# Seven products in place of eight for gate and up in two feed-forwards

## The chip, the cores and the metric

The kernel runs on one core of one Trainium2 chip. The metric is device time in microseconds for one execution, lower is better.

## The reference, cut to what matters

A two-layer backbone over 256 latent tokens and 256 context tokens, model width 1024. Each layer is a half-step SwiGLU feed-forward, a mixer of three kinds of attention, and a second half-step feed-forward; all in float32. The last layer's second feed-forward needs latent tokens alone, so three of the four feed-forwards work on all 512 tokens.

```
def _swiglu(u, w_gate, w_up, w_down):          # u: tokens x 1024, hidden width 2816
    return (jax.nn.silu(u @ w_gate) * (u @ w_up)) @ w_down
h  = h  + 0.5 * g1  * _swiglu(_modulate(_rms_norm(h,  norm_ffn1[l]), sh1,  sc1),  ...)
hc = hc + 0.5 * cg1 * _swiglu(_modulate(_rms_norm(hc, norm_ffn1[l]), csh1, csc1), ...)
```

Shifts, scales and gates (`sh1`, `sc1`, `g1`, ...) come from a product of the silu of a conditioning vector with `w_ada`, 9 x 1024 outputs per layer for each of the two kinds of tokens.

## The kernel before, in words

Activations stand with model rows on the 128 partitions and tokens along the free dimension: `H` is 8 row tiles of 512 columns, latent (`LAT`) in the first 256 and context (`CT`) in the others. Float32 accuracy comes from three matmuls in a reduced format for each product (`mm3`): every weight tile and every activation is split into a high part (a copy by ScalarE) and a low part (a subtraction by VectorE), and high x high, high x low and low x high are added in PSUM. `wload` loads a weight tile of 128 x 1024 by SP's queue into one of three `raw` buffers and splits it into one of four `split` buffers.

`ffn` loops over 22 tiles of 128 hidden rows. `up_one` computes gate and up of one tile: 2 matrices x 8 row tiles x 3 matmuls of 512 columns (256 in the last feed-forward), then `evac` makes silu(gate) x up and its split `G`. `PARTS` groups the tiles by 6, 6, 6 and 4; after the first tile of the next group, `down` projects a whole group: for each of the 8 output tiles `d` a weight load, n x 3 matmuls, and `accum`, in which VectorE adds the gated PSUM half to `H`. The last group is done by halves of the tokens with 256 columns, so that the next norm starts early (`finish`).

Between tiles `run_jobs` issues jobs for the shifts, scales and gates of later stages: each loads 512 KB of `w_adaT` by GpSimd's queue into one of eight `araw` buffers, and VectorE reduces it once for each kind of token (`ada_dve`). The fourth feed-forward has no jobs. The order of work on each engine is set when the program is built, by a scheduler that takes ready instructions in program order; the first tiles and the mixers' steps are ordered by hand. Banks of PSUM: three for `mm`, two for `s` (gates), two for `t` (ups), one for `o`.

Of the kernel before, what the change touches and what calls it, by code (L numbers as in the profile page):

```python
# [13 lines left out]
ALU = mybir.AluOpType  # L14
# [7 lines left out]
PARTS = (6, 6, 6, 4)  # L22
A_H, B_H, C_H = 6, 4, 6
ABUFS = 8
# [36 lines left out]
def hybrid_backbone(ctx: ExitStack, tc: tile.TileContext, I, out):  # L61
# [45 lines left out]
    def late_consts_():  # L107
# [3 lines left out]
        late["maskC"] = const("maskC", [128, 2, 256], I["maskC"])  # L111
# [21 lines left out]
    def mm3(ps, wh, wl, xh, xl, first, last):  # L133
        mm(ps, wh, xh, start=first, stop=False)  # L134
        mm(ps, wh, xl, start=False, stop=False)  # L135
        mm(ps, wl, xh, start=False, stop=last)  # L136

    def proj(ps, sp, U, cols, nk=KT, off=0, k0=0, ks=None):
        for k in ks or range(nk):
            o = off + k * 128  # L140
            mm3(ps, sp[:, 0, o:o + 128], sp[:, 1, o:o + 128], U[0][:, k0 + k, cols], U[1][:, k0 + k, cols],
                k == 0, k == nk - 1)


    def ada_dve(l, ft, cb, ntok, pool):
        raw = pool.tile([128, 1024], F32, tag="araw", name="araw", bufs=ABUFS)
# [3 lines left out]
        for t in range(ntok):  # L150
            stt(scr, raw, 1.0, cb[:, t, :], op0=ALU.mult, op1=ALU.mult, accum_out=ada[l][:, ft, t:t + 1])  # L151
# [84 lines left out]

    def finish(halves, piece, gate, after):
# [23 lines left out]
    def first_tiles(pool, csel, U, src):  # L261
# [14 lines left out]
        def a(p, i):  # L276
# [4 lines left out]
            raw = pool.tile([128, 4, 256], F32, tag="araw", name="araw", bufs=ABUFS)  # L281
# [20 lines left out]
        def w(i):  # L302
            raw = raw_load(src(i), 1024)
            if i < 4:
                t = wp.tile([128, 2, 1024], F32R, tag="split", name="split", bufs=4)
                parts = [(t, 0, 1024)]
            else:
                parts = [(pool.tile([128, 2, 512], F32R, tag="G", name="split0", bufs=10), o, 512) for o in (0, 512)]
            for t, o, n in parts:
                act(t[:, 0, :], raw[:, o:o + n], AF.Copy)  # L310
            sps.append((raw, parts))

        def x(i):
            raw, parts = sps[i]
            for t, o, n in parts:
                tt(t[:, 1, :], raw[:, o:o + n], t[:, 0, :].bitcast(F32), ALU.subtract)
# [19 lines left out]
        def m(i, f):  # L336
            t, o, _ = sps[i][1][f // 4 if i >= 4 else 0]
            wh, wl = (t[:, e, f * 128 - o:f * 128 - o + 128] for e in range(2))
# [11 lines left out]
    def ffn(l, w, halves, pool, U, jobs, after, start=None):  # L350
        both = len(halves) == 2
# [7 lines left out]
        def run_jobs(frac):  # L359
# [589 lines left out]
```

## Time and profile before

| | us |
|---|---|
| median of 3 runs | 1743.18 (1739.81 to 1744.08) |
| the profiled execution | 1742.45 |
| its span, first to last instruction | 1740.5 |
| TensorE busy | 1700.8 (98%) |
| VectorE busy | 1180.0 (68%) |
| ScalarE busy | 718.5 (41%) |
| GpSimd busy | 165.8 (10%) |

The span is what the profiler saw of one execution; its own time stands beside it. Busy time is the time in which an engine had at least one instruction running. Matmuls overlap, so their cost is read from the distance between starts and not from their length.

### The profile page before, as it was taken

The numbers are of one execution on the slowest core, as the hardware profiler recorded it, in microseconds if no ns is written. First come the engines' busy times: TensorE is split into PE (matmuls) and PEld (weight loads), VectorE is DVE, ScalarE is ACT, GpSimd is POOL, SyncE is SP. The second block draws the span as 40 slices with busy tenths as digits, with TensorE's granted clock in tenths as the row PEclk, the third lists the DMA queues.
The fourth block names the chain that finished last, engine by engine and source line by source line (L and its number), as shares of the span: only waits on it lengthen the run. The fifth ranks groups of instructions, "written<-read, shape, count | busy, mean of one in ns | idle before, by whom it ended". The sixth has DMA issues, their size and how long they took to land.

```text
span 1740.5 us, 24756 instructions
## 1 busy us (share of the span) xinstructions
PE 1700.8 (98%) x9572; PEld 1477.5 (85%) x9572; DVE 1180.0 (68%) x2031; ACT 718.5 (41%) x1206; POOL 165.8 (10%) x251
## 2 busy tenths in 40 slices
PE   7999999999999999999999999999999999989997
PEld 4888888889888898888888898888888888889997
DVE  5899963447978869983334599934343787965555
ACT  4322222235888653222222442222222577754443
POOL 0311100012102031100000212100000211100000
PEclk9999999999999999999999999999999999989999
DMA  8877643323223247743333288824332333356663
GB/s 330 309 240 243 197 117 84 110 73 115 58 82 85 75 169 238 236 129 89 108 85 109 63 319 277 321 79 115 85 109 86 99 84 102 109 155 182 182 176 113
DMA packets 76693, 258.37 MB, mean 148 GB/s; under 512 B 8944, under 2 KB 11248, under 8 KB 76192
## 3 DMA queue, kind: packets, MB, share of 16 engines
q1 hardware_dynamic: 54096, 176.72, 33.2%
q0 software_dynamic: 21760, 79.38, 14.3%
q8 instruction: 75, 1.23, 0.3%
q10 hardware_dynamic: 720, 0.69, 0.1%
q14 instruction: 42, 0.34, 0.1%
HBM read 250.47 MB, written 1.05 MB: 145 GB/s over the span
## 4 chain that ended last, share of the span: by engine, by line
PE 89%; DVE 4%; ACT 4%; issue 2%; POOL 1%; DMA 1%; POOLq 0%; DVEq 0%; SPq 0%; ACTq 0%
PE pd L135 8%; PE pd L134 8%; PE pd L136 8%; PE pu L134 8%; PE pu L135 8%; PE pu L136 8%; PE pg L134 8%; PE pg L136 8%; PE pg L135 8%; PE pq L136 1%; PE pq L134 1%; PE pq L135 1%; PE pt L679 1%; DVE split L130 1%; PE pv L580 1%
## 5 line engine op out<-in xcount | busy, mean ns | idle before, releaser
L129 ACT ACTIVATE split<-raw 128x1024 fp32r<-128x1024 f32 (+1 forms) x336 | 332.7, 991 | 546.6 <-PE pu L136 223.2
L130 DVE TENSOR_TENSOR split<-raw,split 128x1024 fp32r<-128x1024 f32 (+1 forms) x336 | 383.9, 1143 | 234.1 <-ACT split L129 233.2
L151 DVE SCALAR_TENSOR_TENSOR ascr<-araw,cb 128x1024 f32<-128x1024 f32 x224 | 273.3, 1220 | 9.9 <-ACT cb L804 7.0
L135 PE MATMUL pd<-G,split 128*128 128x512 f32 (+1 forms) x800 | 272.5, 341 | 0.0
L134 PE MATMUL pd<-G,split 128*128 128x512 f32 (+1 forms) x800 | 271.5, 341 | 0.0
L136 PE MATMUL pd<-G,split 128*128 128x512 f32 (+1 forms) x800 | 271.4, 340 | 0.0
L134 PE MATMUL pg<-Uh,split 128*128 128x512 f32 (+1 forms) x712 | 252.4, 355 | 2.1 <-ACT Uh L225 2.1
L136 PE MATMUL pg<-Uh,split 128*128 128x512 f32 (+1 forms) x712 | 252.3, 354 | 0.0
L135 PE MATMUL pg<-Ul,split 128*128 128x512 f32 (+1 forms) x712 | 252.0, 355 | 0.1
L134 PE MATMUL pu<-Uh,split 128*128 128x512 f32 (+1 forms) x712 | 252.1, 354 | 0.0
L135 PE MATMUL pu<-Ul,split 128*128 128x512 f32 (+1 forms) x712 | 251.9, 354 | 0.0
L136 PE MATMUL pu<-Uh,split 128*128 128x512 f32 (+1 forms) x712 | 251.9, 354 | 0.0
L234 DVE SCALAR_TENSOR_TENSOR H<-pd,ada,H 128x256 f32<-128x256 f32 x272 | 123.3, 479 | 106.9 <-PE pd L136 106.8
L135 PEld LDWEIGHTS pd<-G,split 128*128 128x128 f32 x800 | 151.6, 190 | 17.2
L136 PEld LDWEIGHTS pd<-G,split 128*128 128x128 f32 x800 | 151.4, 190 | 16.9
L134 PEld LDWEIGHTS pd<-G,split 128*128 128x128 f32 x800 | 151.1, 189 | 17.3
L134 PEld LDWEIGHTS pg<-Uh,split 128*128 128x128 f32 x712 | 135.4, 190 | 21.0 <-ACT Uh L225 2.6
L135 PEld LDWEIGHTS pg<-Ul,split 128*128 128x128 f32 x712 | 135.4, 190 | 18.6 <-DVE Ul L226 0.3
L136 PEld LDWEIGHTS pu<-Uh,split 128*128 128x128 f32 x712 | 135.2, 190 | 18.5
L136 PEld LDWEIGHTS pg<-Uh,split 128*128 128x128 f32 x712 | 135.2, 190 | 18.4
L134 PEld LDWEIGHTS pu<-Uh,split 128*128 128x128 f32 x712 | 135.3, 190 | 18.3
L135 PEld LDWEIGHTS pu<-Ul,split 128*128 128x128 f32 x712 | 135.0, 190 | 18.4
(199 smaller groups left out, 2412.6 us busy)
## 6 DMA issues: line engine op xcount, KB each, us to landing
araw<-in_w_adaT POOLq DMA_DIRECT2D x128, 512.0 KB, 5.0
raw<-in_w_ffn_gate SPq DMA_DIRECT2D x88, 512.0 KB, 3.8
raw<-in_w_ffn_up SPq DMA_DIRECT2D x88, 512.0 KB, 3.9
raw<-in_w_ffn_down SPq DMA_DIRECT2D x96, 384.0 KB, 3.2
raw<-in_w_in SPq DMA_DIRECT2D x26, 512.0 KB, 3.5
araw<-in_w_ada SPq DMA_DIRECT2D x16, 512.0 KB, 9.9
raw<-in_w_ffn_down SPq DMA_DIRECT2D x16, 512.0 KB, 3.6
raw<-in_w_out SPq DMA_DIRECT2D x16, 512.0 KB, 3.7
```

Of the source, the lines that this page charges most:

```text
L129: act(sp[:, 0, :n], raw[:, :n], AF.Copy)
L130: tt(sp[:, 1, :n], raw[:, :n], sp[:, 0, :n].bitcast(F32), ALU.subtract)
L134: mm(ps, wh, xh, start=first, stop=False)
L135: mm(ps, wh, xl, start=False, stop=False)
L136: mm(ps, wl, xh, start=False, stop=last)
L151: stt(scr, raw, 1.0, cb[:, t, :], op0=ALU.mult, op1=ALU.mult, accum_out=ada[l][:, ft, t:t + 1])
L234: stt(H[:, d, cols], ps[:, off:off + 256], gate[:, d, half:half + 1], H[:, d, cols], op0=ALU.mult, op1=ALU.add)
L580: mm(ps[:, :n], U[0][:, k, c], s[:, 0, o:o + n], start=(k == 0), stop=False)
L679: nc.tensor.transpose(pt[:, k * 128:(k + 1) * 128], P[t][:, k * 128:(k + 1) * 128], ident)
```

## The change

In the second feed-forward of layer 0 and the first of layer 1 (`FAST`), tiles from 10 on are taken in pairs by `up_fast`. The activations are cut into four blocks (lower and upper four row tiles x latent and context tokens) and the weights of a pair into four blocks (lower and upper rows x gate and up), and the 2 x 2 block product is made of seven block products in place of eight. Each product has 2 x 4 x 3 matmuls of 256 columns. VectorE combines weight blocks before the split and results after the product. Sums of activation blocks (`S1` to `S3`) are made in `forms` after tile 5, `S4` in `last_form` during the first pair, in the place of `U`'s lower context block. The groups become 6, 4, 4, 4, 4, and half of a group's `down` follows each pair.

In these two feed-forwards the additions to `H`, other than those of the last group, are made by a scaled copy on ScalarE and an adding DMA issued by GpSimd (`accum_dma`). The job buffers go from eight to three, seven tenths of the jobs run by tile 8 and the rest with the downs; the jobs of `g2` of layer 1 move from its first to its second feed-forward. The low half of a split tile starts 8 elements (32 bytes) later where its matmuls have 256 columns (`pad`). `maskC` is loaded in each mixer and not once. The rotary code's two work tiles move to another pool with two buffers.

```diff
+FAST = {(0, 2): 10, (1, 1): 10}
+LEAD, EARLY = 4, 0.7
+def parts_of(l, w):
+    return (6, 4, 4, 4, 4) if (l, w) in FAST else (6, 6, 6, 4)
...
-    def wload(src, n=1024):
-        raw = raw_load(src, n)
-        sp = wp.tile([128, 2, 1024], F32R, tag="split", name="split", bufs=4)
-        act(sp[:, 0, :n], raw[:, :n], AF.Copy)
-        tt(sp[:, 1, :n], raw[:, :n], sp[:, 0, :n].bitcast(F32), ALU.subtract)
-        return sp
+    def halves_of(pad):
+        t = wp.tile([128, 2176], F32R, tag="split", name="split", bufs=4)
+        o = 1024 + (8 if pad else 0)
+        return t[:, :1024], t[:, o:o + 1024]
+    def wload(src, n=1024, pad=False):
+        return split(raw_load(src, n), n, pad)
+    def split(raw, n=1024, pad=False):
+        hi, lo = halves_of(pad)
+        act(hi[:, :n], raw[:, :n], AF.Copy)
+        marks["split"] = ins_of(tt(lo[:, :n], raw[:, :n], hi[:, :n].bitcast(F32), ALU.subtract))
+        return hi, lo
...
         for t in range(ntok):
-            stt(scr, raw, 1.0, cb[:, t, :], op0=ALU.mult, op1=ALU.mult, accum_out=ada[l][:, ft, t:t + 1])
+            with tc.issue_after(marks["dve"]) if "dve" in marks else nullcontext():
+                stt(scr, raw, 1.0, cb[:, t, :], op0=ALU.mult, op1=ALU.mult, accum_out=ada[l][:, ft, t:t + 1])
...
+    def accum_dma(ps, off, d, half, gate):
+        cols = (LAT, CT)[half]
+        y = npl.tile([128, 256], F32, tag=("sq", "t")[half], name="y", bufs=2)
+        act(y, ps[:, off:off + 256], AF.Copy, scale=gate[:, d, half:half + 1])
+        nc.gpsimd.dma_start(H[:, d, cols], y, accum_op=ALU.add)
...
-        def run_jobs(frac):
+        def run_jobs(ft):
...
+            if l and not both:
+                frac = ft / 5
+            elif fast == FT:
+                frac = ft / (FT - 3)
+            else:
+                frac = 1 if ft == FT else EARLY * min(1, ft / (fast - 2)) + (1 - EARLY) * downs[0] / 20
...
+        def forms():
+            LO, HI = slice(0, 4), slice(4, 8)
...
+            whole(w1, LO, CT)
+            whole(w2, HI, CT)
+            tt(w2, w1, w2, ALU.add)
+            parts("S1", 0, w2)
+            whole(w3, LO, LAT)
+            tt(w1, w3, w1, ALU.subtract)
+            parts("S3", 1, w1)
+            tt(w3, w2, w3, ALU.subtract)
+            parts("S2", 2, w3)
...
+        def last_form():
...
+            tt(a, U[0][:, 4:8, LAT].bitcast(F32), U[1][:, 4:8, LAT].bitcast(F32), ALU.add)
+            tt(b, fm["S2"][0].bitcast(F32), fm["S2"][1].bitcast(F32), ALU.add)
+            tt(a, a, b, ALU.subtract)
+            act(h, a, AF.Copy)
+            tt(lo, a, h.bitcast(F32), ALU.subtract)
+        def up_fast(ft):
...
+            b11, b12 = fm["w"]
+            nc.sync.dma_start(b11, src(0))
+            nc.sync.dma_start(b12, src(1))
+            b22 = raw_load(src(2), 1024)
+            b21 = raw_load(src(3), 1024)
...
+            A, X, Y, Z = bank("s", "pa"), bank("t", "px"), bank("s", "py"), bank("t", "pz")
+            def prod(ps, w, x, first):
+                sp = split(w, pad=True)
+                xh, xl = fm[x]
+                for i in range(2):
+                    p = ps[:, i * 256:i * 256 + 256]
+                    for k in range(4):
+                        o = i * 512 + k * 128
+                        start = first and i == 0
+                        mm3(p, sp[0][:, o:o + 128], sp[1][:, o:o + 128], xh[:, k], xl[:, k], start and k == 0, k == 3,
+                            not start)
...
+            prod(A, b11, "11", True)
+            p1 = c22
+            act(p1, two(A), AF.Copy)
+            tt(b11, b12, b11, ALU.subtract)
+            tt(t2, b22, b11, ALU.subtract)
+            prod(X, t2, "S2", True)
+            marks["dve"] = ins_of(tt(u2, two(X), p1, ALU.add))
+            prod(Y, b11, "S1", True)
+            tt(b12, b22, b12, ALU.subtract)
+            prod(Z, b12, "S3", True)
+            u3 = pool.tile([128, TOK], F32, tag="sil", name="u3", bufs=2)
+            tt(two(u3), two(Z), u2, ALU.add)
+            marks["dve"] = ins_of(tt(c22, two(Y), two(u3), ALU.add))
+            if ft == fast:
+                last_form()
+            prod(A, b21, "12", False)
+            sil = pool.tile([128, TOK], F32, tag="sil", name="sil", bufs=2)
+            act(sil[:, LAT], A[:, :256], AF.Silu)
+            tt(sil[:, LAT], sil[:, LAT], A[:, 256:], ALU.mult)
+            tt(t2, t2, b21, ALU.subtract)
+            X = bank("t", "px2")
+            prod(X, t2, "22", True)
+            tt(u3, u3, X, ALU.subtract)
+            act(sil[:, CT], u3[:, :256], AF.Silu)
+            tt(sil[:, CT], sil[:, CT], u3[:, 256:], ALU.mult)
+            prod(Y, b22, "S4", False)
+            tt(u2, two(Y), u2, ALU.add)
+            act(cc[:, 0], cc[:, 0], AF.Silu)
+            marks["dve"] = ins_of(tt(cc[:, 0], cc[:, 0], cc[:, 1], ALU.mult))
...
+            for v in (sil, cc[:, 0]):
+                g = pool.tile([128, 2, TOK], F32R, tag="G", name="G", bufs=gbufs)
+                act(g[:, 0], v, AF.Copy)
+                tt(g[:, 1], v, g[:, 0].bitcast(F32), ALU.subtract)
...
                     for h in halves:
-                        accum(ps, h * 256, d, h, gate)
+                        (accum_dma if fast < FT else accum)(ps, h * 256, d, h, gate)
+                    if p0 + n >= fast:
+                        downs[0] += 1
+                        marks["dve"] = marks["split"]
+                        run_jobs(fast)
...
+                elif ft >= fast:
+                    G[ft], G[ft + 1] = up_fast(ft)
+                    j += 2
...
-                run_jobs((p0 + j) / (FT - 3))
+                run_jobs(min(p0 + j, fast))
+                if fast < FT and p0 + j == fast - LEAD:
+                    forms()
                 if pend is not None:
-                    down(*pend, False)
-                    pend = None
+                    slow = ft < fast
+                    down(*pend, False, range(KT) if slow else range(0, 4) if j == 2 else range(4, 8))
+                    if slow or j == n:
+                        pend = None
...
-                jobs = ada_jobs(1, ("shm", "scm"), pool) + ada_jobs(1, ("gm", "sh2", "sc2", "g2"), pool, 1)
+                jobs = ada_jobs(1, ("shm", "scm"), pool, 2, 3) + ada_jobs(1, ("gm", "sh2", "sc2"), pool, 1, 3)
...
-                jobs = []
+                jobs = ada_jobs(1, ("g2",), pool, 1)
```

## Rows read from the trace of the kernel before

**Rows 1.** The page: the chain that ended last, shares by engine.

```profile
PE 89%; DVE 4%; ACT 4%; issue 2%; POOL 1%; DMA 1%; POOLq 0%; DVEq 0%; SPq 0%; ACTq 0%
```

**Rows 2.** Busy time by stage: stretch and length, busy us and instructions by engine, granted clock, DMA share, GB/s.

```profile
630.00:965.00 335.00, 334.49 (x1570) 280.89 (x1570) 208.05 (x321) 96.63 (x126) 18.32 (x34) 1.00 0.49 150
1000.00:1330.00 330.00, 330.00 (x1539) 276.89 (x1540) 204.08 (x311) 92.42 (x118) 25.83 (x49) 1.00 0.55 179
...
1540.00:1715.00 175.00, 175.00 (x1451) 175.00 (x1450) 103.58 (x139) 80.07 (x113) 0.00 (x0) 0.99 0.61 178
```

**Rows 3.** Timeline of TensorE: start us, length us; a block of 512 columns.

```profile
785.09 0.39 PE L134 MATMUL pg<-Uh,split 128*128 128x512 f32 x1
...
790.53 0.39 PE L134 MATMUL pu<-Uh,split 128*128 128x512 f32 x1
```

**Rows 4.** Timeline of TensorE: a block of 256 columns, last feed-forward.

```profile
1602.72 0.28 PE L134 MATMUL pg<-Uh,split 128*128 128x256 f32 x1
...
1605.61 0.28 PE L134 MATMUL pu<-Uh,split 128*128 128x256 f32 x1
```

**Rows 5.** Timeline of TensorE: transposes and mixed matmuls of the first mixer.

```profile
506.04 1.04 PE L679 MATMUL pt<-ident,P 128*128 128x128 f32 x8
...
507.15 0.40 PE L135 MATMUL pq<-Ul,split 128*128 128x512 f32 x1
...
507.62 0.40 PE L134 MATMUL pq<-Uh,split 128*128 128x512 f32 x1
...
508.70 0.38 PE L698 MATMUL pt<-ident,P 128*128 128x128 f32 x2
...
509.04 0.28 PE L642 MATMUL S<-kd,q 128*128 128x256 f32 x1
...
509.98 0.28 PE L688 MATMUL po<-pth,vab 128*128 128x256 f32 x1
```

**Rows 6.** Groups of VectorE by line and shape: count, busy us, mean ns.

```profile
L130 DVE TENSOR_TENSOR split<-raw,split 128x1024 fp32r<-128x1024 f32 x232 | 284.7, 1227 | 171.6 <-ACT split L129 171.5
L151 DVE SCALAR_TENSOR_TENSOR ascr<-araw,cb 128x1024 f32<-128x1024 f32 x224 | 273.3, 1220 | 9.9 <-ACT cb L804 7.0
...
L130 DVE TENSOR_TENSOR split<-raw,split 128x768 fp32r<-128x768 f32 x104 | 99.3, 955 | 62.5 <-ACT split L129 61.7
...
L372 DVE TENSOR_TENSOR sil<-sil,pu 128x512 f32<-128x512 f32 x63 | 43.1, 685 | 93.7 <-PE pu L136 93.7
...
L151 DVE DVE_READ_ACCUMULATOR ascr<-araw,cb 128x1 f32 x224 | 18.2, 81 | 0.0
...
L372 DVE TENSOR_TENSOR sil<-sil,pu 128x256 f32<-128x256 f32 x22 | 9.3, 421 | 11.6 <-PE pu L136 11.6
```

**Rows 7.** Busy time of a stretch with VectorE full, and of a changed one.

```profile
87.00:217.00 130.00, 130.00 (x575) 107.67 (x574) 128.90 (x210) 35.02 (x44) 17.33 (x33) 1.00 0.73 227
...
830.00:965.00 135.00, 135.00 (x597) 111.81 (x596) 50.90 (x65) 35.10 (x44) 0.00 (x0) 1.00 0.36 102
```

**Rows 8.** Groups of ScalarE by line and shape.

```profile
L129 ACT ACTIVATE split<-raw 128x1024 fp32r<-128x1024 f32 x232 | 244.9, 1057 | 344.0 <-PE pu L136 140.1 <-PE pd L136 123.7 <-issue 35.5
...
L373 ACT ACTIVATE G<-sil 128x512 fp32r<-128x512 f32 x66 | 40.9, 622 | 41.4 <-DVE sil L372 41.2
L371 ACT ACTIVATE sil<-pg 128x512 f32<-128x512 f32 x63 | 37.7, 598 | 200.5 <-PE pg L136 200.5
...
L584 ACT ACTIVATE vab<-pv 128x256 fp32r<-128x256 f32 x8 | 3.1, 382 | 7.6 <-PE pv L582 7.6
```

**Rows 9.** GpSimd's issues, and transfers: KB each, median us to landing (the third from 87 to 217).

```profile
L538 POOL DMA_DIRECT2D kd<-kd x20 | 10.6, 532 | 125.1 <-DVE kd L537 115.5 <-issue 4.0 <-PE po L689 2.4
...
raw<-in_w_ffn_gate SPq DMA_DIRECT2D x88, 512.0 KB, 3.8
...
kd<-kd POOLq DMA_DIRECT2D x20, 256.0 KB, 3.2
...
araw<-in_w_adaT POOLq DMA_DIRECT2D x33, 512.0 KB, 4.8
```

More of the change, by code (lines that the diff above doesn't have):

```diff
@@ L350, in ffn @@
     def ffn(l, w, halves, pool, U, jobs, after, start=None):
+        fast = FAST.get((l, w), FT)
+        gbufs = 8 if fast < FT else 10
         both = len(halves) == 2
@@ L393, in up_two, with whole, parts @@
             return [evac(pss[0], pss[1]), evac(pss[2], pss[3])]
+        fm = {}
+        def forms():
+            LO, HI = slice(0, 4), slice(4, 8)
+            rows = lambda t: t.rearrange("p (a b) -> p a b", a=4)
+            block = [pool.tile([128, 1024], F32R, name=f"S{i}", bufs=1) for i in range(6)]
+            w1, w2 = fm["w"] = [pool.tile([128, 1024], F32, name=f"w{i}", bufs=1) for i in range(2)]
+            w3 = pool.tile([128, 1024], F32, tag="t2", name="w3", bufs=1)
+            def whole(t, k, c):
+                with tc.issue_after(marks["dve"]):
+                    tt(rows(t), U[0][:, k, c].bitcast(F32), U[1][:, k, c].bitcast(F32), ALU.add)
+            def parts(n, i, t):
+                h, lo = block[2 * i:2 * i + 2]
+                act(h, t, AF.Copy)
+                tt(lo, t, h.bitcast(F32), ALU.subtract)
+                fm[n] = (rows(h), rows(lo))
+            whole(w1, LO, CT)
[7 more added lines that the diff above has]
+            parts("S2", 2, w3)
+            for n, k, c in (("11", LO, LAT), ("12", HI, LAT), ("22", HI, CT)):
+                fm[n] = (U[0][:, k, c], U[1][:, k, c])
@@ new lines, in last_form @@
+        def last_form():
+            h, lo = fm["S4"] = U[0][:, 0:4, CT], U[1][:, 0:4, CT]
+            rows = lambda t: t.rearrange("p (a b) -> p a b", a=4)
+            a, b = (rows(pool.tile([128, 1024], F32, tag="araw", name="s4", bufs=3)) for _ in range(2))
+            tt(a, U[0][:, 4:8, LAT].bitcast(F32), U[1][:, 4:8, LAT].bitcast(F32), ALU.add)
[3 more added lines that the diff above has]
+            tt(lo, a, h.bitcast(F32), ALU.subtract)
@@ L395, in ffn, with down @@
         G = {}
         off = [0]
-        def down(p0, n, last):
+        downs = [0]
+        def down(p0, n, last, ds=range(KT)):
             if not last:
-                for d in range(KT):
-                    sp = wload(wd[l, :, off[0]:off[0] + n * 128], n * 128)
+                for d in ds:
+                    sp = wload(wd[l, :, off[0]:off[0] + n * 128], n * 128, not both)
                     off[0] += n * 128
@@ L425, in ffn @@
         p0 = 0
-        for pi, n in enumerate(PARTS):
+        parts = parts_of(l, w)
+        for pi, n in enumerate(parts):
             j = 0
```

105 lines of the change are left out of this document (59 added, 46 removed).

## The prediction

> **What bounds the kernel now.** I read the page first: TensorE is busy for 1700.8 us, 98% of the span, as the table above has it, and the chain that ended last is 89% TensorE [rows 1]. Then the table of stages over the two feed-forwards that change (630 to 965 and 1000 to 1330 us) and the last one: TensorE is busy for 334.5 of 335 and 330 of 330 us at a granted clock of 1.00 (2.4 GHz), VectorE for 62%, ScalarE for under 30% [rows 2]. So a microsecond of matmul saved there is a microsecond of the kernel, as long as nothing else starts to hold TensorE.
>
> The duration of a matmul (0.39 us at 512 columns, 0.28 at 256) is no price: matmuls overlap. The price is the interval between starts. Between the starts of two blocks of 24 matmuls of 512 columns lie 790.53 - 785.09 = 5.44 us, 226.7 ns each [rows 3]; for 256 columns, 1605.61 - 1602.72 = 2.89 us, 120 ns each [rows 4]. Each is the column time at 2.4 GHz (213.3; 106.7) plus 13.3 ns: halving the columns does not halve the price.
>
> **The change: matmuls.** A pair of tiles from 10 on costs 2 tiles x 2 matrices x 8 x 3 = 96 matmuls of 512 columns = 21.76 us. Seven products of 2 x 4 x 3 are 168 matmuls of 256 columns, at 120 ns 20.16 us. That is 7.4% less, not the 12.5% of the arithmetic. There are six pairs in each of two feed-forwards: 1152 become 2016 matmuls, 261.1 us against 241.9, a saving of 19.2 us. The other parts of the down projection are cut 6,4,4,4,4 for 6,6,6,4: 18 tiles of 512 columns and 4 in halves in both cases, no difference.
>
> The second term is quieter. Where matmuls have 256 columns, the low half of a split weight tile now begins 32 bytes further on, in the new products and in 2736 other matmuls: 1584 of the last feed-forward, 576 of the last down parts of the other three, 384 of the output projections, 192 of the second mixer's queries. No row has that offset. The interval of 256 columns isn't always 120: in the first mixer, where weights come from other tiles, starts at 509.04 to 509.98 are 117.5 ns apart over eight [rows 5]. The floor I take from matmuls whose columns no longer set the pace: two transposes of 128 columns (53 ns each) take 0.38 us and eight take 1.04, so six more cost 0.66 and they start 110 ns apart [rows 5]. From the other side, a 512-column stream there has starts at 507.15 and, two on, 507.62, 235 ns apart, 8 over the steady value [rows 5]; so 128 for 256 columns. At 110 the change saves 261.1 - 221.8 + 27.4 = 66.7 us, at 117.5 24.2 + 6.8 = 31.1, at 120 19.2, at 128 it saves 3.1 and loses 21.9 elsewhere. I take 117.5, which rows show for this shape and which lies nearer to the 120 of the same tiles than the floor does.
>
> The Trainium skill, page "TensorE: Matmul & The Clock Gate", section "Back-to-back issue gap", gives the isolated gap as columns / 2.4 plus 2.5 ns: 215.8 and 109.2. By it the products alone would save 248.6 - 220.1 = 28.5 us. The trace has 226.7 and 120 for these loads, and the measurement decides.
>
> **VectorE.** One pair asks of it seven splits and four weight combinations of 1024 at 1.227 us, 13.5; six operations of 512 at 0.685 on products and gate, and two of 256 at 0.421, 5.0; two low halves of G (0.685), 1.4; four down splits of 512 at 0.685, 2.7: 22.6 us [rows 6]. The eight accumulations into `H` are gone from it. Jobs of the modulation (1.220 + 0.081 per token): three tenths of 32 jobs with two tokens and of 40 with one are spread over 20 downs, four per pair, 5.0 and 3.1 us. Their operations are only put in order behind marked ones. That makes 27.6 and 25.7 us against 19.74 + 10.88 = 30.6 of TensorE; now VectorE is busy for 38% there [rows 7]. Does TensorE stand a full VectorE? From 87 to 217 us VectorE is busy for 128.9 of 130 us and TensorE never waits [rows 7]; so the low bound is nothing. There the filling work was needed by nobody soon, while here every product waits for a combination and a split. The first pair also builds S4, four operations of 1.227: 32.5, 1.9 over. I price VectorE's lateness at 5 us: 2 for that pair and 0.3 for each of the others, a choice near the lower bound, where the row is; the upper one stands with the rivals.
>
> Building S1 to S3 is nine operations of 1.227 and three copies, 11 and 3 us, after tile 5. Tiles 0 to 9 with the six-tile down (144 matmuls) last 10 x 10.88 + 32.6 = 141 us and ask 20 splits (24.5), gate and G (13.7), down splits of 768 (7.6), the forms (11) and 70% of the jobs (60): 117, 83%, under the 99% above. Cost: nothing; without that cover 14 per feed-forward.
>
> **ScalarE, GpSimd, the queues.** ScalarE has per pair seven copies of 1.057, four of 0.62 for downs, 2.6 for gates and G, A's first copy at 0.598 and eight scaled copies at 0.382: 16 of 30.6 us, hidden [rows 8]. Each of these eight is followed by an add issued by GpSimd (0.53 us of its time, idle in this stretch [rows 7, 9]). The nearest transfer between SBUF tiles is 256 KB and lands in 3.2 us [rows 9]; ours has 128 KB, but also reads its target. I take 3.2. Each half has two buffers, so a copy waits for the add two downs back: 0.38 + two issues of 0.53 + 3.2 = 4.6 us against 2 x 2.72 = 5.44 of matmuls. It fits with 0.8 to spare.
>
> The page "SBUF — State Buffer" of the Trainium skill, section "Who interferes with whom", speaks against such adds: GpSimd cannot write descriptors while VectorE runs a two-port operation. Where VectorE is 99% busy, GpSimd's loads of 512 KB landed in 4.8 us, so nothing of it shows [rows 9].
>
> SP loads per pair four tiles of 512 KB (3.8 us) and four of 256; the first two wait for the splits of the third and fourth product of the pair before, some twenty us ahead of their use. Behind them in SP's order stand the down tiles and the other two, in three buffers, two of which a pair holds; a slot turns in 3.8 + 1.06 + 1.23 = 6.1 us with the down phase of 10.9 to do it. I take nothing. The jobs of g2 move to the last feed-forward: eight loads, eight operations of 1.3, a load and activation of the conditioning row; VectorE has 71 us free there [rows 2]. The mask moves to both mixers, one load each, needed late. Both at nothing; uncovered 12 and 5 us.
>
> **Sum.** 24.2 + 6.8 - 5 = 26 us off the profiled execution's 1742.45 (span 1740.5), 1716.4; that execution lies 0.7 under the median, so 1717.
>
> **The rivals.** *The offset does nothing.* For it: the 120 holds through whole blocks on split tiles [rows 4]. 1742.45 - 19.2 + 5 + 0.7 = 1729.
>
> *The offset brings the floor.* 66.7 - 5 off: 1681. Against it: no run of 256 columns below 117 for long.
>
> *The adds come late (the other side).* If reading the target doubles the landing to 6.4 us, a buffer turns in 7.9, 2.4 us over 5.44. ScalarE then stands on the third down of every half with the next splits queued behind it, and TensorE runs out of weights: 12 x 2.4 = 29 us, 1717 + 29 = 1746, no gain. It decides from a landing of 4.0 us, costs 12 us for each further one, and eats the gain at 6.2. Against it: three PSUM banks and ready products give TensorE other work. A job's load waiting for one of three (not eight) buffers ahead in GpSimd's order would do the same.
>
> *VectorE becomes the bound.* If each product exposed its own split (a ScalarE copy of 1.06 before 1.23), a pair's product phase took 7 x 1.06 + 19.8 = 27.2 for 19.7 us; half of that 7.5, over 12 pairs, is 45 us: 1757. It decides above 2.2 us a pair.
>
> *The offset or the new layout slows all 256-column matmuls* to 128: 1743.15 - 3.1 + 21.9 + 5 = 1767.
>
> **How the numbers follow.** Mine 0.42, no effect of the offset 0.22, floor 0.08, late adds 0.13, VectorE 0.10, slower matmuls 0.05. A measurement of this kernel tells about 0.3%, 5 us, from no change: 1738 and 1748. Faster has the first three (0.72) and the milder part of late adds and VectorE (0.05): 0.77; same 0.08; slower 0.15. The likeliest is 1717, its own range 1705 to 1727. From 1690 to 1748 the range leaves out the floor, the slow matmuls and most of VectorE's case, 0.20. Gains are bounded by the floor, 1681.
>
> **What would show it.** In the new profile: 168 matmuls of 256 columns per pair, starts 117.5 ns apart (120 would be the first rival, and the last feed-forward then stays as long as it is); TensorE's idle in the fast stretches about 5 us in all, most in the first pairs, before a split of VectorE; VectorE 85 to 90% busy there; adds landing in about 3.2 us and ScalarE not waiting on one; the first ten tiles free of gaps. I am wrong if ScalarE's waits name a DMA, if idle per pair passes 2 us, or if the interval lies outside 114 to 120.

## The result, and the profile after

The changed kernel takes 1753.97 us (median of 4 runs, 1752.97 to 1755.13); the kernel before, run beside it, 1743.12. The ratio is 1.0066, with a 95% interval of 1.0048 to 1.0083: it became slower, by 11 us, where 1717 was forecast. The profiled execution has a span of 1752.3 us against 1740.5.

The chain that ended last, on the page of the changed kernel, answers to [rows 1]:

```profile
PE 55%; issue 22%; DVE 9%; POOL 6%; ACT 4%; DMA 2%; POOLq 0%; DVEq 0%; SPq 0%; ACTq 0%
```

TensorE's share of the chain fell from 89% to 55%. This row alone doesn't tell how much TensorE lost. In the pairs the chain runs along GpSimd's adds and long pieces called issue, one of them from 850.45 us for 15.94 us, while TensorE is busy throughout; and e14, the fastest run below, still has 65% and 17% issue:

```profile
850.45 15.94 issue
```

```profile
PE 65%; issue 17%; DVE 7%; POOL 6%; ACT 4%; DMA 1%; POOLq 0%; DVEq 0%; SPq 0%; ACTq 0%
```

Where TensorE loses time is read from busy time by stage (stretch and length; busy us and instructions of TensorE, its weight loads, VectorE, ScalarE, GpSimd; granted clock, DMA share, GB/s), which answers to [rows 2] and [rows 7]:

```profile
690.00:750.00 60.00, 49.94 (x212) 40.58 (x211) 48.15 (x68) 19.59 (x32) 16.51 (x23) 0.91 0.76 215
750.00:830.00 80.00, 80.00 (x487) 71.88 (x487) 61.24 (x76) 33.69 (x49) 13.30 (x17) 1.00 0.55 147
830.00:965.00 135.00, 135.00 (x946) 126.55 (x945) 109.25 (x142) 68.94 (x111) 31.51 (x38) 1.00 0.59 147
...
1045.00:1120.00 75.00, 59.26 (x253) 48.24 (x252) 61.15 (x91) 22.03 (x32) 19.43 (x30) 0.89 0.80 240
...
1185.00:1330.00 145.00, 145.00 (x1022) 136.22 (x1021) 113.76 (x138) 74.75 (x118) 38.14 (x46) 1.00 0.62 155
```

In the pairs, which the second row (with the tiles just ahead of them), the third and the fifth hold, nothing is lost: TensorE is busy for 80 of 80, 135 of 135 and 145 of 145 us, VectorE for 76 to 81%. The loss stands in the first and fourth row: 49.94 of 60 us with a granted clock of 0.91, 59.26 of 75 with 0.89. Both stretches hold the six-tile down, in the tiles that the change hardly touches. The last feed-forward lost as well (175.00 of 175 before):

```profile
1540.00:1715.00 175.00, 167.71 (x1375) 166.87 (x1376) 111.65 (x163) 80.09 (x113) 5.47 (x10) 0.97 0.66 201
```

The waits of TensorE (for what; us in all, times, longest) name the releaser:

```profile
PE pd L153 <- DVE split L146: 25.8, 2, 15.7
...
PE pg L153 <- DVE split L146: 3.3, 1, 3.3
```

Two waits for the low half of a down split make 25.8 us, one in each of the two feed-forwards that changed; a third, in the last feed-forward, makes 3.3. The timeline of VectorE (start, length) around the longer one shows why the split was late. L146 is the subtraction that makes the low half, L169 a modulation product, L443 to L458 the six sums S1 to S3 with their parts:

```profile
1063.75 0.96 DVE L146 TENSOR_TENSOR split<-raw,split 128x768 fp32r<-128x768 f32 x1
...
1071.79 1.22 DVE L443 TENSOR_TENSOR w<-Uh,Ul 128x1024 f32<-128x1024 f32 x1
1072.93 1.22 DVE L169 SCALAR_TENSOR_TENSOR ascr<-araw,cb 128x1024 f32<-128x1024 f32 x1
...
1080.92 1.22 DVE L448 TENSOR_TENSOR S<-w,S 128x1024 fp32r<-128x1024 f32 x1
...
1090.48 1.22 DVE L448 TENSOR_TENSOR S<-w,S 128x1024 fp32r<-128x1024 f32 x1
1093.25 1.22 DVE L169 SCALAR_TENSOR_TENSOR ascr<-araw,cb 128x1024 f32<-128x1024 f32 x1 [1.56 <-DMA araw<-in_w_adaT]
...
1097.20 1.22 DVE L169 SCALAR_TENSOR_TENSOR ascr<-araw,cb 128x1024 f32<-128x1024 f32 x1
...
1098.35 0.96 DVE L146 TENSOR_TENSOR split<-raw,split 128x768 fp32r<-128x768 f32 x1
```

ScalarE had made the high half of that second split long before:

```profile
1078.58 0.83 ACT L145 ACTIVATE split<-raw 128x768 fp32r<-128x768 f32 x1
```

From the first split of the down at 1063.75 to the second at 1098.35 VectorE is hardly idle: 16 modulation products, nine operations of the sums, four of gate and G of two tiles. Three products wait for their own loads on top, 1.56 us the longest. The high half was ready at 1079.4, so the split stood 19 us behind work that stood ahead of it in VectorE's order. Then TensorE goes on at half its rate:

```profile
1099.36 0.80 PE L153 MATMUL pd<-G,split 128*128 128x512 f32 x1 [15.71 <-DVE split L146]
...
1100.38 0.63 PE L152 MATMUL pd<-G,split 128*128 128x512 f32 x1
1100.80 0.63 PE L153 MATMUL pd<-G,split 128*128 128x512 f32 x1
...
1103.59 0.40 PE L151 MATMUL pd<-G,split 128*128 128x512 f32 x1
1103.82 0.39 PE L152 MATMUL pd<-G,split 128*128 128x512 f32 x1
```

After 15.71 us of waiting, starts are 0.42 us apart (512 columns at 1.2 GHz); at 1103.59 they are 0.23 apart again. What the intervals behind the two long waits have beyond 226.7 ns adds up to 1.6 and 2.0 us.

Of the terms of the forecast, two matmuls 96 apart in a pair give the new interval, and page and list of transfers give the adds [rows 4, 8, 9]:

```profile
878.44 0.28 PE L151 MATMUL pa<-Uh,split 128*128 128x256 f32 x1
...
889.80 0.28 PE L151 MATMUL pa<-Uh,split 128*128 128x256 f32 x1
```

```profile
L260 POOL DMA_DIRECT2D H<-y x128 | 112.2, 1032 | 190.6 <-ACT y L259 186.5
...
araw<-in_w_adaT POOLq DMA_DIRECT2D x128, 512.0 KB, 4.4
...
H<-y POOLq DMA_DIRECT2D x128, 128.0 KB, 3.5
```

11.36 us for 96 matmuls are 118.3 ns, against 120 in [rows 4] and 117.5 forecast. An add of 128 KB lands in 3.5 us (the median; 2.6 to 9.4; 3.2 taken), and GpSimd is busy for 1.03 us with issuing one (0.53 taken).

**The 11.8 us between the two spans.** Products: 2016 x 118.4 ns = 238.7 for 261.2 us, 22.5 gained. Offset elsewhere: 2736 x 1.6 ns = 4.4 gained. Intervals of 512 columns beyond 226.7 ns, summed over all starts of the stages: 12.4 us lost in the first changed feed-forward and 18.3 in the second. Last feed-forward: about 5.6 lost (3.5 of wait beyond an interval, 0.6 at a shorter wait 4 us ahead of it, some 1.5 of lower clock). That makes 9.4. Of the other 2.4, some 1.3 stand at a mixer's value split and 1.2 at the start of the second changed feed-forward, where matmuls of 256 columns are 213 ns apart (1.2 GHz) from 1001.8 to 1004.2 us.

### The profile page after: what moved, and what is told of

It is laid out like the page before. It is cut to its first block, busy times and chain, and to the rows that moved or that the text cites. A ratio compares the mean times of both kernels' runs of the same rounds, so it can differ in the third digit from the quotient of the medians.

```text
span 1752.3 us, 27258 instructions
## 1 busy us (share of the span) xinstructions
PE 1682.2 (96%) x10436; PEld 1499.8 (86%) x10436; DVE 1308.8 (75%) x2133; ACT 827.0 (47%) x1419; POOL 281.3 (16%) x381
## 4 chain that ended last, share of the span: by engine, by line
PE 55%; issue 22%; DVE 9%; POOL 6%; ACT 4%; DMA 2%; POOLq 0%; DVEq 0%; SPq 0%; ACTq 0%
PE pd L153 5%; PE pd L151 5%; PE pd L152 5%; POOL H L260 5%; PE pg L153 4%; PE pg L151 4%; PE pu L151 4%; PE pu L153 4%; PE pg L152 4%; DVE ascr L169 4%; PE pu L152 4%; PE pq L153 1%; PE pq L151 1%; PE pq L152 1%; DVE split L146 1%
## 5 line engine op out<-in xcount | busy, mean ns | idle before, releaser
L146 DVE TENSOR_TENSOR split<-raw,split 128x1024 fp32r<-128x1024 f32 (+2 forms) x328 | 356.0, 1087 | 190.5 <-ACT split L145 188.9
L145 ACT ACTIVATE split<-raw 128x1024 fp32r<-128x1024 f32 (+2 forms) x328 | 310.5, 948 | 378.8 <-PE pu L153 132.0
L153 PE MATMUL pd<-G,split 128*128 128x512 f32 (+1 forms) x800 | 272.9, 342 | 25.8 <-DVE split L146 25.8
L169 DVE SCALAR_TENSOR_TENSOR ascr<-araw,cb 128x1024 f32<-128x1024 f32 x224 | 273.4, 1220 | 5.3 <-DMA araw<-in_w_adaT 3.2
L153 PE MATMUL pg<-Uh,split 128*128 128x512 f32 (+1 forms) x520 | 178.3, 343 | 3.3 <-DVE split L146 3.3
L151 PE MATMUL pg<-Uh,split 128*128 128x512 f32 (+1 forms) x520 | 178.2, 343 | 2.6 <-ACT Uh L243 2.1
L151 PE MATMUL pu<-Uh,split 128*128 128x512 f32 (+1 forms) x520 | 177.5, 341 | 0.0
L152 PE MATMUL pg<-Ul,split 128*128 128x512 f32 (+1 forms) x520 | 177.3, 342 | 0.1
L153 PE MATMUL pu<-Uh,split 128*128 128x512 f32 (+1 forms) x520 | 177.3, 341 | 0.0
L152 PE MATMUL pu<-Ul,split 128*128 128x512 f32 (+1 forms) x520 | 177.0, 340 | 0.0
L165 POOL DMA_DIRECT2D araw<-in_w_adaT x128 | 69.4, 543 | 554.5 <-DVE ascr L169 500.0
L260 POOL DMA_DIRECT2D H<-y x128 | 112.2, 1032 | 190.6 <-ACT y L259 186.5
L153 PEld LDWEIGHTS pg<-Uh,split 128*128 128x128 f32 x520 | 99.5, 191 | 14.5 <-DVE split L146 3.5
L151 PEld LDWEIGHTS pg<-Uh,split 128*128 128x128 f32 x520 | 99.4, 191 | 14.1 <-ACT Uh L243 2.6
L152 PEld LDWEIGHTS pg<-Ul,split 128*128 128x128 f32 x520 | 99.5, 192 | 11.1 <-DVE Ul L244 0.3
L151 PEld LDWEIGHTS pu<-Uh,split 128*128 128x128 f32 x520 | 99.0, 190 | 10.9
```

Of the source, the lines that this page charges most:

```text
L145: act(hi[:, :n], raw[:, :n], AF.Copy)
L146: marks["split"] = ins_of(tt(lo[:, :n], raw[:, :n], hi[:, :n].bitcast(F32), ALU.subtract))
L151: mm(ps, wh, xh, start=first, stop=False, skip_group_check=go_on)
L152: mm(ps, wh, xl, start=False, stop=False, skip_group_check=go_on)
L153: mm(ps, wl, xh, start=False, stop=last, skip_group_check=go_on)
L165: nc.gpsimd.dma_start(raw, I["w_adaT"][l, :, ft * 1024:(ft + 1) * 1024])
```

## The experiments

The first theory (Theory 1): VectorE's work ahead of the six-tile down holds its splits. The rivals: the adding DMAs are at fault, by landing late or by holding GpSimd and ScalarE (Theory 2); the products, the offset or other parts cost more than reckoned (Theory 3). The share is `EARLY`, the part of the jobs that is run ahead of tile 10, 0.7 in the change; the sums are S1 to S3, made after tile 6 in the change (`LEAD`). All times are medians, beside the kernel before on the same chip (1742.32, 1741.47, 1742.58 and 1742.07 in the four sets of runs).

| run | us | ratio to before, 95% |
|---|---|---|
| e1, sums after tile 8 | 1740.50 | 0.9998 (0.9983 to 1.0013) |
| e2, six-tile down's adds on VectorE | 1762.24 | 1.0114 (1.0099 to 1.0129) |
| e3, share 0.45 | 1729.60 | 0.9932 (0.9912 to 0.9952) |
| e4, no offset | 1761.66 | 1.0111 (1.0093 to 1.0129) |
| e5, no products | 1749.32 | 1.0042 (1.0027 to 1.0057) |
| e6, share 0.45, gate jobs a tile later | 1723.64 | 0.9895 (0.9881 to 0.9908) |
| e7, as e6, share 0.55, sums after tile 8 | 1736.13 | 0.9963 (0.9951 to 0.9975) |
| e8, share 0.45, no adding DMA | 1753.62 | 1.0071 (1.0058 to 1.0085) |
| e9, as e6, sums after tile 8 | 1734.10 | 0.9954 (0.9938 to 0.9970) |
| e10, no products, gate jobs a tile later | 1744.75 | 1.0010 (1.0001 to 1.0020) |
| e11, as e6, share 0.58 | 1731.76 | 0.9945 (0.9926 to 0.9964) |
| e12, as e6, share 0.30 | 1743.75 | 1.0008 (0.9999 to 1.0017) |
| e13, as e6, share 0.7, sums between splits | 1726.52 | 0.9918 (0.9901 to 0.9935) |
| e14, as e13, share 0.58 | 1721.63 | 0.9883 (0.9868 to 0.9897) |
| e15, as e6, share 0.58 in the first alone | 1721.77 | 0.9882 (0.9868 to 0.9897) |

### Less of VectorE's work ahead of the down: e1 and e3

```diff
-LEAD, EARLY = 4, 0.7
+LEAD, EARLY = 2, 0.7        # e1: the sums after tile 8, behind the six-tile down
+LEAD, EARLY = 4, 0.45       # e3: 45% of the jobs ahead of tile 10
```

> S1 to S3 are built two tiles later, after the six-tile down has been issued. Theory 1 (VectorE's backlog: the sums and the jobs stand in front of the first down's splits in VectorE's order): each of the two long waits of TensorE in tiles 6 to 7, 10.4 and 16.1 us with some 2 us at the lower clock behind each, shrinks by the 11 us of the sums; the time goes from 1754 to between 1728 and 1734. Theory 2 (the adding DMAs and the loads queued on GpSimd hold the down): the waits stay, 1754. Theory 3 (the seven products gain less than their count says): the waits shrink but the time stays above 1743.

> 45% of the jobs instead of 70% before the products. Theory 1: by tile 7 VectorE has 7 jobs of 2.6 us less in the first of the two feed-forwards and 9 operations of 1.3 us less in the second, so the waits of 10.4 and 16.1 go to nothing and about 4; in the pairs VectorE's work rises to 31.8 and 28.3 us for 30.8 of TensorE, up to 1 us a pair in the first: 1730 to 1738. Theory 2: the waits stay, 1754 or above.

Both long waits are gone in both runs, so neither the sums nor the share of 0.7 makes them alone: they need both. e3 is at 1729.6, 24 us under the change and inside the expected range. e1 missed its own: 1740.5, since the sums, taken out of the way of the down, now stand ahead of tile 9 and the first pair; there TensorE stops for 4.4 us at 773 and again at the start of the pair.

### The adding DMAs: e2 and e8

```diff
-                        (accum_dma if fast < FT else accum)(ps, h * 256, d, h, gate)
+                        (accum_dma if fast < FT and p0 + n >= fast else accum)(ps, h * 256, d, h, gate)   # e2
+                        accum(ps, h * 256, d, h, gate)                                                    # e8, share 0.45
```

> The six-tile down adds to H on VectorE as before the change; the later downs keep the adding DMA. Theory 1 (VectorE's backlog): the two waits stay at 10 and 16 us or grow by a few, since VectorE gets 16 operations of 0.48 us more in that stretch; 1752 to 1760. Theory 2 (the adding DMAs): the two waits vanish, 1726 to 1730.

> The version with 0.45 of the jobs ahead of tile 10, all adding DMAs replaced by VectorE's own adds from PSUM (128 of 421 ns, 54 us of VectorE, 27 in each of the two feed-forwards). First theory (adding DMAs are worth what VectorE lacks before tile 10, where the six-tile down has 16 of the 64 adds of each feed-forward, 6.7 us, and nothing in the pairs, where VectorE is 81% busy): some 2 to 8 us more than 1729.6, so 1732 to 1738. Rival (the adding DMAs cost on GpSimd's queue, where each is issued in 1.03 us, and by landing late): 1724 to 1728. Second rival (VectorE runs over in the pairs as well): 1740 or more.

Taking the adding DMAs away makes both kernels slower, so Theory 2 falls as the cause of the long waits. In e2, 2 us above the range of Theory 1, the long waits grow to 11.1 and 18.3 us, and four more operations stand ahead of the second split. e8 is 24 us slower than e3, as its second rival had it and not its first theory: the adds in the down bring back waits there (gaps of 2.3 and 2.8 us in each), and the pairs lose too (below).

### Products, offset and the rest: e4, e5 and e10

```diff
-        o = 1024 + (8 if pad else 0)
+        o = 1024                     # e4
-FAST = {(0, 2): 10, (1, 1): 10}
+FAST = {}                            # e5, e10
-                frac = ft / 5
+                frac = max(0, ft - 1) / 5   # e10, and e6
```

> The low half of a split tile stands right behind the high half everywhere. If the 32 bytes are what took the 256-column interval from 120 to 118.4 ns, it returns to 120 and the 4752 matmuls concerned cost 7.6 us more: 1762. If the new layout did it, 1754.

> The table of feed-forwards with the seven-product scheme is empty, so that all parts are 6, 6, 6 and 4 tiles, no adding DMA and no form is made, and the old spreading of jobs holds; what is left of the change is the 32-byte offset, the marks that hold the modulation products back, the mask load in the mixer and the gate jobs of the last feed-forward five tiles long. First theory (the scheme saves TensorE time and pays it away in the waits ahead of the six-tile down): the offset gives 1.65 ns on 2736 matmuls, 4.5 us, and the early gate jobs of the last feed-forward cost the 5.5 us seen there (3.6 of wait, 0.7, some 1.2 of lower clock), so about 1743, from 1739 to 1747. Rival (something of the surroundings, such as the marks or three buffers in place of eight for the modulation tiles, takes the time): 1749 or more.

> No feed-forward uses the scheme, and the gate jobs of the last feed-forward begin a tile later. Against the version at 1723.6 us this prices the scheme itself, where its waits are gone. First theory: the last feed-forward's wait goes here too, 5 to 6 us less than 1749.3, so 1743 to 1745; the scheme is then worth some 20 us, near the 22.5 us that its products save by the measured intervals. Rival (part of what the surroundings cost in the run without products was another effect of the gate jobs or chance of that chip): 1738 or less, and the scheme worth 15 us or less.

e4 is 7.7 us above the change, as (2016 + 2736) x 1.6 ns = 7.6 has it: the offset does what its interval shows, and 256-column products without it stand at 120 ns. In e5 the rival was nearer: 1749.3. With the gate jobs a tile later, e10 has 1744.8, still 2 above before in spite of 4.4 from the offset. So all that surrounds the scheme costs some 6.5 us; of that the waits show 1.3 at each mixer, where a value split waits 1.8 us (0.5 and 0.3 before), 1.0 at a down split of the first feed-forward (128.7 us) and 1.7 at a split of the last one (1557.9 us). Against e6 the scheme itself is worth 1744.75 - 1723.64, corrected for the kernel before in the two sets 20 us, near the 22.5 of its intervals. Theory 3 falls for the products and the offset; for the rest it holds, with these 6.5 us.

### The gate jobs of the last feed-forward: e6

> The version with 0.45 of the jobs ahead of tile 10 and, besides, the gate jobs of the last feed-forward begin a tile later (share (tile - 1) / 5 in place of tile / 5). First theory (the same thing on a small scale: VectorE's products stand ahead of the splits of the first tiles): the 3.6 us wait there and the lower clock behind it go, 4 to 5.5 us less than 1729.6, so 1724 to 1726. Rival (the wait there comes from the load of the first weights or from the norm ahead of it, and only shows at the split): no change, 1729 to 1731.

6 us less than e3: at the small scale, too, modulation products ahead of a split made the wait of 3.3 us. A smaller wait stays in the last feed-forward, 1.4 us in e6 and 2.8 in e14, for a split's high half; in e14 ScalarE had waited 1.72 us for the load of that weight tile. In e6 the two stretches of the six-tile down, which answer to the first and fourth row by stage above, are:

```profile
690.00:750.00 60.00, 59.98 (x265) 49.31 (x265) 38.51 (x48) 23.51 (x38) 16.13 (x20) 1.00 0.70 183
...
1045.00:1120.00 75.00, 74.98 (x331) 61.73 (x331) 54.61 (x72) 28.39 (x43) 18.68 (x25) 1.00 0.73 198
```

TensorE is busy throughout, at full clock.

### How full VectorE may be in the pairs: e7, e9 and e12

```diff
-LEAD, EARLY = 4, 0.45     # e6
+LEAD, EARLY = 2, 0.55     # e7
+LEAD, EARLY = 2, 0.45     # e9
+LEAD, EARLY = 4, 0.3      # e12
```

> Gate jobs of the last feed-forward a tile later, the six sums after tile 8 in place of tile 6, and 0.55 of the jobs ahead of tile 10. First theory (each piece of VectorE work ahead of the six-tile down counts, the sums as much as the jobs): the sums behind the down free 11 us of VectorE there and 0.10 of 24 and 40 jobs puts back 6 to 10, so the down stays without long waits; 1722 to 1727. Rival (the sums so late make the first pair late): 2 to 5 us more at each first pair, 1728 to 1736.

> As the version at 1723.6 us (0.45 of the jobs ahead of tile 10, gate jobs of the last feed-forward a tile later), with the six sums after tile 8 in place of tile 6. It parts the two edits of the run that came out at 1736.1. First theory (the sums, 11 us of VectorE, are late for the first pair when they stand after tile 8): waits of the first products for splits and a lower clock behind them in both feed-forwards, 1729 to 1735. Rival (it was the share 0.55): 1722 to 1726.

> As the version at 1723.6 us with a share of 0.3, so that 22 of 32 and 28 of 40 jobs stand with the pairs. First theory: the tiles before 10 have room already with 0.45 and gain nothing more; in the pairs VectorE goes from 83% busy in 850 to 975 us by 5 jobs of 2.44 us in 250 us to some 88%, still short of the bound: 1722 to 1727. Rival (the pairs have no such room, since each product waits for sums that stand behind the jobs): 1729 or more.

e7 fell to its rival, and e9 shows which edit did it: with the sums after tile 8 and the share of e6 it is 1734, so the sums are late for the first pair. e12 fell to its rival as well. The stretch from 850 to 975 us, four pairs' worth, in e6, e12 and e8:

```profile
850.00:975.00 125.00, 124.95 (x876) 116.88 (x875) 104.43 (x147) 61.77 (x103) 34.71 (x43) 1.00 0.65 165
```

```profile
850.00:975.00 125.00, 120.13 (x825) 111.63 (x826) 110.40 (x153) 62.72 (x99) 30.82 (x40) 0.99 0.67 173
```

```profile
850.00:975.00 125.00, 118.10 (x815) 109.90 (x816) 114.62 (x168) 49.15 (x68) 3.71 (x7) 0.99 0.41 125
```

In this stretch TensorE loses nothing with VectorE 84% busy (104.43 of 125), 4.9 us with 88% and 6.9 us with 92%. These are three runs and no threshold, for not all of the loss is VectorE's. The wait table of e12 says where:

```profile
PE px L151 <- ACT split L145: 6.6, 5, 3.5
```

The high half of the second product's split comes late five times, up to 3.5 us. Three causes show. At 819 us in the second pair, the low half stands behind a modulation product and a combination on VectorE (a gap of 1.2 us). In the next pair the combination `t` is ready at 848.3, on VectorE's timeline,

```profile
847.06 1.23 DVE L506 TENSOR_TENSOR t<-raw,w 128x1024 f32<-128x1024 f32 x1
```

but ScalarE, on its own, stands on the scaled copy of an add, waits 3.09 us for the adding DMA that holds the buffer, and copies `t` only then; TensorE's gap is 2.6 us:

```profile
850.12 0.47 ACT L259 ACTIVATE y<-pd,ada 128x256 f32<-128x256 f32 x1 [3.09 <-DMA H<-y]
...
851.13 1.05 ACT L145 ACTIVATE split<-t 128x1024 fp32r<-128x1024 f32 x1
```

That is the late add of the forecast's rival, in a pair whose job loads share the queue. The same stands in e3 at 846 us: ScalarE waits 3.97 us for such a DMA, and TensorE's gap behind it is 1.8 us. The longest wait, 3.5 us at 1186.6, has a third cause. VectorE itself waits for the load of a job that stands ahead of the pair's combinations,

```profile
1181.79 1.23 DVE L169 SCALAR_TENSOR_TENSOR ascr<-araw,cb 128x1024 f32<-128x1024 f32 x1 [1.80 <-DMA araw<-in_w_adaT]
```

and `t` is ready only at 1185.4. So the jobs can't all go to the pairs. But e12 also had a wait of 2.7 us in the first six-tile down, with fewer jobs ahead of it than e6, which had none. Amount alone can't explain that.

### Amount or order: e11, e13, e14 and e15

The distance between the first and the second split of the six-tile down on VectorE, and TensorE's gap for that second split:

| run, feed-forward | distance, us | gap, us |
|---|---|---|
| change, first | 27.6 | 10.4 |
| change, second | 34.6 | 16.1 |
| e2, first / second | 30.6 / 38.6 | 11.1 / 18.3 |
| e11, second | 27.6 | 9.2 |
| e12, first | 22.5 | 2.7 |
| e6, both | 14.3, 14.2 | none |
| e11, first | 13.4 | none |
| e13, both | 7.8, 7.8 | none |

Where there is a gap, it is the distance less 17 to 20 us; the shorter distances have none. These 17 to 20 us are what TensorE has in hand: in the change it worked from the end of the first split, 1064.7, to 1083.65. And the distance doesn't follow the share: 0.58 gives 13.4 in one feed-forward and 27.6 in the other. It goes with whether the scheduler that writes VectorE's order puts the second split amid the sums (e3, e6, e15, the first of e11, the second of e12: 11.9 to 14.3 us) or behind all of them (the change, e2, the second of e11, the first of e12: 22.5 to 38.6). In e6 it stands amid them:

```profile
1053.42 0.95 DVE L146 TENSOR_TENSOR split<-raw,split 128x768 fp32r<-128x768 f32 x1
...
1060.75 1.22 DVE L443 TENSOR_TENSOR w<-Uh,Ul 128x1024 f32<-128x1024 f32 x1
...
1067.58 0.95 DVE L146 TENSOR_TENSOR split<-raw,split 128x768 fp32r<-128x768 f32 x1
...
1074.19 1.23 DVE L448 TENSOR_TENSOR S<-w,S 128x1024 fp32r<-128x1024 f32 x1
...
1076.47 0.96 DVE L146 TENSOR_TENSOR split<-raw,split 128x768 fp32r<-128x768 f32 x1
```

Three runs part order from amount. e13 keeps the share of 0.7 and makes the sums in six steps, each behind a split of the down:

```diff
-                if fast < FT and p0 + j == fast - LEAD:
-                    forms()
+                if fast < FT and p0 + j == fast - LEAD:
+                    steps = forms()          # a generator now: six steps, with yield between them
...
                     for h in halves:
                         (accum_dma if fast < FT else accum)(ps, h * 256, d, h, gate)
+                    if fast < FT and p0 + n < fast:
+                        marks["dve"] = marks["split"]
+                        next(steps, None)
```

e14 is the same with a share of 0.58; e15 is e6 with 0.58 in the first of the two feed-forwards and 0.45 in the second.

> As the version at 1723.6 us with a share of 0.58 in place of 0.45, between it and the 0.7 of the change. Ahead of the six-tile down stand 17 of 32 and 21 of 40 jobs (0.7: 20 and 25; 0.45: 13 and 16). First theory (a backlog of VectorE that must be worked off before the splits, so the wait falls by the products taken away): 3 jobs of 2.44 us fewer than with 0.7 in the first of the two feed-forwards, 5 products of 1.22 us fewer in the second, so waits of about 3 and 10 us in place of 10.4 and 16.1, and 1736 to 1742 us. Rival (an all-or-nothing wait, as for a buffer or a load): both waits whole, 1746 or more, or none, 1722 to 1727.

> Share 0.7 as in the change, the same sums, the gate jobs of the last feed-forward a tile later; only the order differs: the six sums are made in six steps, one after each of the first six splits of the six-tile down, and the products that follow are marked to stand behind that split. First theory (order: the wait is the distance between the first and the second split of the down on VectorE, less some 18 us that TensorE has in hand; here no more than six or seven short operations stand between two splits): both long waits gone, 1720 to 1729. Rival (amount: VectorE has more work ahead of tile 10 than time, in whatever order): waits of 5 to 15 us spread over the down or moved to tile 9 and the first pair, 1736 to 1748.

> The order of the run with the sums between the splits, with a share of 0.58. First theory (with the order mended, the share hardly counts between 0.45 and 0.7): within 4 us of that run, 1719 to 1728. Rival (amount): 5 to 10 us under that run.

> The version at 1723.6 us with a share of 0.58 in the first of the two feed-forwards alone, where the run with 0.58 had no wait and 3 us less lost than the run with 0.45, and 0.45 in the second, where 0.58 gave a wait of 9.2 us. First theory (order; a share matters by where the second split falls among the sums, in each feed-forward by itself): no long wait in either, 1719 to 1723. Rival (the missing wait with 0.58 was chance): a wait of 3 us or more in the first, 1725 to 1730.

e11 landed between its theories: the wait of the second feed-forward came as reckoned (9.2 for 10), that of the first not at all (3 expected), which the distances explain. e13 is at 1726.5, as its first theory had it: with the sums and the share of the change it is 27 us under the change, of which 6 are the gate jobs. In its first down the first three splits are 7.8 and 10.1 us apart; then VectorE's timeline has a split every 4.3 us, with products and sums between:

```profile
713.09 0.95 DVE L146 TENSOR_TENSOR split<-raw,split 128x768 fp32r<-128x768 f32 x1
...
715.19 1.22 DVE L448 TENSOR_TENSOR S<-w,S 128x1024 fp32r<-128x1024 f32 x1
...
717.47 0.95 DVE L146 TENSOR_TENSOR split<-raw,split 128x768 fp32r<-128x768 f32 x1
...
719.49 1.22 DVE L443 TENSOR_TENSOR w<-Uh,Ul 128x1024 f32<-128x1024 f32 x1
...
721.77 0.95 DVE L146 TENSOR_TENSOR split<-raw,split 128x768 fp32r<-128x768 f32 x1
```

The two stretches of the down:

```profile
690.00:750.00 60.00, 60.00 (x266) 49.71 (x265) 50.28 (x71) 23.89 (x37) 19.98 (x27) 1.00 0.88 246
...
1045.00:1120.00 75.00, 69.95 (x302) 57.40 (x301) 57.54 (x81) 25.71 (x40) 22.75 (x32) 0.98 0.83 246
```

The first is full, with VectorE busier (50.28 of 60) than in the change (48.15), where TensorE lost 10. That is order, not amount. The second still loses 5, at the seventh split, and the timeline shows why:

```profile
1085.76 1.22 DVE L169 SCALAR_TENSOR_TENSOR ascr<-araw,cb 128x1024 f32<-128x1024 f32 x1 [1.00 <-DMA araw<-in_w_adaT]
...
1092.08 1.22 DVE L169 SCALAR_TENSOR_TENSOR ascr<-araw,cb 128x1024 f32<-128x1024 f32 x1 [1.60 <-DMA araw<-in_w_adaT]
...
1093.23 0.95 DVE L146 TENSOR_TENSOR split<-raw,split 128x768 fp32r<-128x768 f32 x1
```

The split at 1093.23 stands behind a product that waited 1.60 us for its load, after another that waited 1.00, in a stretch with a DMA share of 0.83. With the smaller share of e14 that wait is gone too: 1721.6. That is 4.9 us under e13, between the 4 of its first theory and the 5 to 10 of its rival, so with the order mended the amount still counts a little. e15 has 1721.8 in the other way, as its first theory had it. By the median both are the fastest kernels here, 1.2% under the kernel before, though the interval of e6 overlaps theirs.

## Why the prediction was wrong

**The step that failed** is the one on tiles 0 to 9: "Tiles 0 to 9 with the six-tile down (144 matmuls) last 10 x 10.88 + 32.6 = 141 us and ask [...] 117, 83%, under the 99% above. Cost: nothing". The sum of work was right (VectorE is busy for 117.2 us from 638 to 783 us). The step averaged over 141 us, while the jobs come evenly up to tile 8 and the sums after six tiles, and both stand ahead of the down's second split in VectorE's order. TensorE has 17 to 20 us in hand there; the order asked 27.6 and 34.6. Cost: 12.4 and 18.3 us, lower clock included, in place of nothing (the same step had 14 for each feed-forward "without that cover", which is about what came). The row that seemed to cover it, VectorE 99% busy from 87 to 217 us without a wait of TensorE [rows 7], tells that a full VectorE can be harmless where splits stand between the filling work (at most 8.1 us apart on VectorE there), not that it is so in any order.

**The last feed-forward** was also priced at nothing, by VectorE's 71 free us there [rows 2]. It cost 5 to 6: the jobs began with the first tile, whose splits had no lead.

**Right in kind:** the interval (118.3 to 118.4 for 117.5, so 22.5 us for 24.2 on the products and 4.4 for 6.8 on the others); the pairs, where 5 us of lateness were taken and none shown, VectorE at 76 to 81% where 85 to 90 was forecast; the adds, 3.5 us for 3.2. Two of these are partly luck. The 117.5 was taken from matmuls without the offset; six others of 256 columns in the same mixer start 120 ns apart (505.32 to 505.92 us), so the row didn't point to 118.3. And with the order mended, a share of 0.58 and the gate jobs a tile later the change gives 1721.6, near the 1717, because errors partly cancel: the intervals gain 26.9 for 31.0 us, and the 6.5 us of the surroundings, priced at nothing, stand where 5 were taken for VectorE's lateness in the pairs. GpSimd's issue of an add takes 1.03 us for 0.53.

**The rivals.** Late adds: ScalarE's waits do name the adding DMA, as the forecast's own test asked,

```profile
ACT y L259 <- DMA H<-y: 17.9, 13, 3.2
```

yet in the change TensorE is busy throughout the pairs, and e2 and e8, with fewer such adds or none, are slower. The mechanism is real all the same: it makes small waits that e3 and e12 have left at the start of a pair. There the adds land in 4.7 and 4.5 us (medians), past the 4.0 at which the forecast let it decide, and cost less (gaps of 1.8 and 2.6 us) than the forecast's 12 us for each microsecond past it. The forecast's doubt about descriptors written beside VectorE found nothing either: with VectorE 76 to 81% busy in the pairs the adds' median is 3.5 us. VectorE as the bound was the right engine in the wrong place; its form in the pairs shows in e8 (92% of VectorE) and for a part in e12 (88%), which the change doesn't reach. The offset doing nothing, bringing the floor or slowing the matmuls are excluded by the interval.

**Left open.** Why the scheduler places the second split amid the sums in one build and behind them in another wasn't tried; that the distance goes with the place is read from the orders alone, and e13 shows that moving the sums takes the wait away.

## What to carry to other kernels

An engine's busy share over a stage doesn't tell of a wait inside it: follow the order on that engine from one operation that the bounding engine needs to the next, and compare that distance with the work that the bounding engine has in hand. When work is added to a helper engine in one block, put it between the operations that feed the bound, a step behind each, rather than ahead of them. And price moved filler at the place where it lands: the jobs moved out of the full feed-forward cost 6 us at the start of one where VectorE had 71 us free.

## What the hardware showed beside

A second half of a stationary tile pair that begins 32 bytes later brings the interval of 256-column matmuls from 120 to 118.4 ns (e4, without it, is back at 120). No run gives the offset to matmuls of 512 columns. The Trainium skill gives in "TensorE: Matmul & The Clock Gate", section "Back-to-back issue gap", columns / 2.4 plus 2.5 ns for one matmul alone, 109.2 here; the trace has 9 ns more, and the rule has no term for the place of the weights.

VectorE slows down beside GpSimd's arithmetic. In e6's first mixer, the timeline shows two additions on GpSimd and two pairs of equal operations of VectorE:

```profile
404.16 2.74 POOL L762 TENSOR_TENSOR bias<-bias,maskC 128x512 f32<-128x512 f32 x2 [2.65 <-DMA bias<-in_rpb]
404.23 2.95 DVE L244 SCALAR_TENSOR_TENSOR Ul<-t,ada,Uh 128x256 fp32r<-128x256 f32 x2
...
409.02 0.87 DVE L244 SCALAR_TENSOR_TENSOR Ul<-t,ada,Uh 128x256 fp32r<-128x256 f32 x2
```

The pair beside GpSimd's additions took 2.95 us, the pair after them 0.87. In the Trainium skill, "SBUF — State Buffer", section "Who interferes with whom", VectorE's tensor_tensor with both inputs in SBUF contends with GpSimd's reads; the operation here, its relative with a scalar, agrees. The additions came 2.6 us later than in the kernel before, behind loads of which the mask's is now the first, and the value split behind them made TensorE wait 1.7 us.
